# Three feed-forward blocks on the unnormed input instead of two, and the token mixer's loads and masks issued ahead of its layer norm

## The chip, the cores and the metric

The kernel is one program on one core of a Trainium2 chip. The metric is the time of one execution in microseconds (us). Weights come from HBM through the DMA queues while the core computes; TensorE (PE in the profile) does the matrix products, VectorE (DVE), ScalarE (ACT) and GpSimd (POOL) the elementwise work, SyncE (SP) issues most of the DMAs.

## The reference

One inference step of a decoder trunk with two layers, on 512 prompt positions and 8 x 4 sample positions, 544 columns in all, all in fp32. Cut to what matters here:

```
h = rmsnorm(x, norm1_g);  proj = h @ w_in            # 1024 -> 12 projections
A: gated delta rule     B: short gated convolution
C: out_c = window_attn_banded(cq, ck, cv, sinks)      # window 128, softmax with sinks
D: du  = gelu(d_u);  dvn = layernorm(gelu(d_v), d_ln_g, d_ln_b)
   wm  = where(tril, d_ws, 0)
   out_d = du * (einsum('gts,bcsgd->bctgd', wm, dvn) + d_bias)
x = x + concat(out_a, out_b, out_c, out_d) @ w_out
h2 = rmsnorm(x, norm2_g)
gate = causal_dwconv(h2 @ ffn_w_gate)                 # width 3, D_FF = 2816
x = x + (silu(gate) * (h2 @ ffn_w_up)) @ ffn_w_down
```

The states of the convolutions, the delta rule and the window caches are outputs too.

## The kernel before

**Numbers.** Activations lie with the channels on the 128 partitions and the 544 positions as columns. An fp32 product is made of three products of rounded parts: each operand is split into a high part (`xh`, `wh`) and a low part (`xl`, `wl`), and hi·hi, lo·hi and hi·lo are added in PSUM. A weight arrives as `wr`; ACT makes `wh` (L745), DVE makes `wl` (L747).

**Who sets the order.** PE's order is laid down when the program is built, by a planner (class `Order`). The main line yields after pieces of matrix products (`pj_*` are the projections); side generators yield a delay in microseconds, or an event that another one marks with a delay, and the planner, which adds up estimated PE time, takes whichever is due. The table `LAT` adds a delay to single steps of a generator. Side generators of layer l are `a` (delta rule), `c` (attention, `mix_c`), `d` (token mixing, `mix_d`), `e` (the sample positions' attention) and `n` (the layer norm of `dv`). The order of the other engines follows from a tile scheduler, so a step that moves on PE moves instructions on ACT and DVE as well.

**PSUM.** The pool `pss` has two buffers, which attention's scores (`psc`), its transposes (`ptr`), its products (`pov`), and token mixing's products (`pmx` for the prompt, `pmd` for the samples) take in turn. The pool `pmm` has two as well: projections, and in the feed-forward part `pgt` (gate) and `pup` (up) of one block after the other. A tile can be written again only when the last reader of the buffer's former content is done.

**Attention, one block of 128 queries.** PE writes the scores `psc`; DVE adds the mask (L1348), takes the maximum and its negative `nm` (L1254); ACT takes the exponentials (L1260) and, once the sum is inverted, scales (L1268); PE transposes into two tiles `ptr` (L441); ACT copies each to `pt` (L1363); PE multiplies with the values, `pov`.

**Token mixing (`mix_d`).** It waits for the event `dv{l}` (layer norm of `dv` done, `dvn` and `dvd` the results), loads the mixing weights `wmt`, masks them on POOL (L1379), loads and masks a small copy `wm4` (`wm`) for the samples (L1382), loads `dbias`, and then for each of two halves has PE multiply (`pmx`, `pmd`) and DVE add the bias and multiply with `du` (L1399).

**Feed-forward, 22 blocks of 128 channels per layer.** The first ones, `f < RAW`, use the input before the norm (`raw`): the products are made with the split `xs`, and the inverse norm `rstd` is multiplied in afterwards by DVE (L1713 and L1714 on the gate, L1716 before, and L1719 with the up product). Blocks up to 4 (`plain`) use the normed input in "forms": `fm.halves(kp)`, issued after block 0, makes the normed tiles `hn` (DVE, L578), and splits them into `f1h`, `f2h`, `f3h` (ACT, L586 and L515) and `f1l`, `f2l`, `f3l` (DVE, L587 and L516), for four values of kp; a plain block's gate goes from PSUM to SBUF by ACT (L1728, L1729), and its up product is multiplied in by DVE (L1734). Blocks from 5 on (`seven`) use seven products of half size where there would be eight, and for this need sums of the forms (`fm.sums()`: `fu`, `fv` on DVE, split into `f4`, `f5`), issued after block `RAW`.

Of the kernel before, what the change touches and what calls it, by code (L numbers as in the profile page):

```python
# [28 lines left out]
NK = DM // 128  # L29
EPS = 1e-6  # L30
FGROUPS = [(0, 5), (5, 11), (11, 17), (17, 22)]
RAW, PLAIN = 2, 5
P0 = 512 - HT


# [238 lines left out]
def _unhost(r):  # L274
# [8 lines left out]
    def conv(a, k, n):  # L283
# [19 lines left out]

LAT = {
    "a00": {
        3: 1.60, 13: 15.62, 14: 3.75, 15: 2.87, 16: 1.87, 17: 3.23, 18: 1.78, 19: 2.03, 34: 1.52,
    },
    "a01": {
        3: 3.96, 4: 1.12, 10: 2.64, 24: 0.84,
    },  # L310
    "a10": {
        3: 1.56, 13: 15.67, 14: 3.68, 15: 2.79, 16: 3.85, 17: 1.45, 25: 1.33, 36: 0.47, 42: 1.13,
    },
    "a11": {
        3: 3.59, 6: 3.32, 13: 1.06, 28: 0.70, 35: 0.30,
    },
    "c0": {
        1: 1.19, 2: 4.34, 5: 7.17, 6: 0.65, 7: 2.67, 8: 3.40,
    },
    "c1": {  # L320
        1: 0.81, 2: 4.06, 5: 7.68, 6: 0.61, 7: 15.38, 10: 1.48,
    },
    "d0": {
        4: 6.53,
# [90 lines left out]
def _body(ctx, tc, I, O, depth=DEPTH, dump=None):  # L415
# [7 lines left out]
    od = Order()  # L423

    def mm(out, lhsT, rhs, **kw):
        k, m, n = lhsT.shape[0], lhsT.free_size(), rhs.free_size()
        if lhsT.dtype == F32R:
            c = max(n, 256) / 2400.0 + 0.0025
        else:
            c = 4 * max(n, m) / 2400.0  # L430
            if k <= 32 and m <= 32:
                c *= 0.74
            elif k <= 64 and m <= 64:
                c *= 0.72
        od.spend(c, n * k / 128.0 * (1 if lhsT.dtype == F32R else 4))
        nc.tensor.matmul(out, lhsT, rhs, **kw)  # L436
# [9 lines left out]
    def bc(ap, axis, n):  # L446
        u = ap.unsqueeze(axis)
        shp = list(u.shape)
        shp[axis] = n
        return u.to_broadcast(shp)  # L450
# [16 lines left out]
    def n5(nm, w=571):  # L467
        return p5.tile([128, w], F32, tag="w5", name=nm)

    def nx(nm, shape, dt=F32):  # L470
        return slabs.tile(shape, dt, tag="s5", name=nm)

    def ncc(nm, shape):
        return pc.tile(shape, F32, tag="c2", name=nm)
# [4 lines left out]
    def ps(nm, shape):  # L479
        return pss.tile(shape, F32, tag="ps", name=nm)  # L480

    def psmm(nm):
        return pmm.tile([128, 1024], F32, tag="mm", name=nm)
# [16 lines left out]
    def C(nm, a=None, b=None):  # L500
        o, n = _COFF[nm]
        if a is None:
            return cst[:, o:o + n]
        return cst[:, o + a:o + b]
# [8 lines left out]
    def split(src, nm):  # L513
        hi, lo = nx(nm + "h", [128, T], F32R), nx(nm + "l", [128, T], F32R)
        act(hi, src, AF.Copy)  # L515
        tt(lo, src, hi.bitcast(F32), op=ALU.subtract)  # L516
        return hi, lo
# [232 lines left out]
    def wnext():  # L750
        while len(wready) < 3:
            n = len(wready)
            wprep()
            if len(wready) == n:
                break
        return wready.pop(0)
# [28 lines left out]
    def dmp(nm, ap):  # L785
        if dump is not None and nm in dump:
            nc.gpsimd.dma_start(dump[nm], ap)

    def bs(ap):
        return ap.rearrange("p (b t) -> p b t", b=DB)  # L790
# [582 lines left out]


    def mix_d(l, L):
        yield ("ev", f"dv{l}")
        wmt = nx("wmt", [128, 4, 128])
        nc.sync.dma_start(wmt, I["wmt"][l])
        pool.tensor_tensor(wmt, wmt, bc(C("tri"), 1, 4), op=ALU.mult)  # L1379
        wm4 = ncc("wm4", [32, 4, 32])  # L1380
        nc.sync.dma_start(wm4, I["wm4"][l])
        pool.tensor_tensor(wm4, wm4, bc(C("udc")[0:32], 1, 4), op=ALU.mult)  # L1382
        dbias = ncc("dbias", [128, 2, 128])
        nc.sync.dma_start(dbias, I["dbias"][l])
        for i in range(2):
            yield ("ev", f"u{l}{i}")
            pmx = ps("pmx", [128, 4, 128])
            for n in range(4):
                for a in range(2):
                    gr = 2 * i + a  # L1390
                    mm(pmx[hs[a], n], L.dvn[n // 2][:, n % 2, 64 * gr:64 * gr + 64], wmt[:, gr],
                       start=True, stop=True)
            pmd = ps("pmd", [128, ND])
            for a in range(2):
                gr = 2 * i + a
                mm(pmd[hs[a]], L.dvd[0:ND, 64 * gr:64 * gr + 64], wm4[:, gr], start=True, stop=True,
                   tile_position=(0, 64 * a))
            mx_ = n5("mx_", T)
            tt(mx_[:, 0:SEQ].rearrange("p (n t) -> p n t", n=4), pmx, bc(dbias[:, i], 1, 4), op=ALU.add)  # L1399
            tt(bs(mx_[:, SEQ:T]), bs(pmd), bc(dbias[:, i, 0:DS], 1, DB), op=ALU.add)  # L1400
            tt(mx_, mx_, L.du[i], op=ALU.mult)
            dmp(f"od{i}", mx_)
            L.cat[6 + i] = split(mx_, f"d{i}")
            yield 1.0
        od.mark(f"catD{l}", 3.5)


    def main():
# [7 lines left out]
        def xk(k):  # L1416
            return xr[k // 2][:, k % 2, :]
# [33 lines left out]
        for l in range(depth):  # L1451
# [53 lines left out]
            for c in range(5):  # L1505
# [5 lines left out]
                dv = dvn[c // 2][:, c % 2] if c < 4 else dvd[0:ND]  # L1511
# [15 lines left out]
            def normed_dv():  # L1527
                yield ("ev", f"nd{l}")
                with tc.issue_after(L.du_ins):
                    for c, (dv, r0) in enumerate(dvs):  # L1530
                        ts(dv, dv, mv[0:r0, c, 0:1], rs[0:r0, c:c + 1], op0=ALU.subtract, op1=ALU.mult)
                        pool.tensor_tensor(dv, dv, lnr[0:r0, 0], op=ALU.mult)
                        pool.tensor_tensor(dv, dv, lnr[0:r0, 1], op=ALU.add)
                nc.sync.dma_start(O["cvs"][l], dvd[0:ND])
                od.mark(f"dv{l}", 8.0)

            od.spawn(normed_dv(), f'n{l}')
            yield 0.0
# [165 lines left out]
            def raw(f, first):  # L1704
                p = psmm("pgt")
                yield from gemm(p, wnext(), xs)
                pu = psmm("pup")
                gu = gemm(pu, wnext(), xs)
                if first:
                    yield next(gu)  # L1710
                    nrm.finish()
                pb, dec = gate_in(f)
                tt(pb[:, 2:2 + SEQ], pflat(p, 0, SEQ), rstd[:, 0:SEQ], op=ALU.mult)  # L1713
                tt(dec[:, :, 2:6], bs(pflat(p, SEQ, T)), bs(rstd[:, SEQ:T]), op=ALU.mult)  # L1714
                sl = gate_out(f, pb, dec)
                tt(sl, sl, rstd, op=ALU.mult)  # L1716
                yield 0.0
                yield from gu
                tt(sl, sl, pflat(pu), op=ALU.mult)  # L1719
                hid[f] = split(sl, "hd")  # L1720
                yield 0.0

            def plain(f):

                p = psmm("pgt")
                yield from gemm_halves(p, wnext(), fm.whole())
                pb, dec = gate_in(f)
                act(pb[:, 2:2 + SEQ], pflat(p, 0, SEQ), AF.Copy)  # L1728
                act(dec[:, :, 2:6], bs(pflat(p, SEQ, T)), AF.Copy)  # L1729
                sl = gate_out(f, pb, dec)  # L1730
                yield 0.0
                pu = psmm("pup")
                yield from gemm_halves(pu, wnext(), fm.whole())
                tt(sl, sl, pflat(pu), op=ALU.mult)  # L1734
                hid[f] = split(sl, "hd")
                yield 0.0
# [37 lines left out]
            for kind, i, f0, f1 in FFN_ORDER:  # L1774
                if kind == "plain":
                    yield from raw(i, i == 0) if i < RAW else plain(i)
                    if i == 0:
                        for kp in range(NK // 2):
                            fm.halves(kp)
                    elif i == RAW:  # L1780
                        with tc.issue_after(fm.end.ins):
                            fm.sums()
                    continue
                if kind == "seven":
                    yield from seven(i)
                    continue
                m, last = i, f1 == NF
                hd = [hid[f] for f in range(f0, f1)]
                if last and l + 1 == depth and m >= NK - 2:
                    if m == NK - 2:  # L1790
                        yield from finale(xk, xr, nnrm, hd)
                    continue
                p = psmm("pdn")
                yield from gemm(p, wnext(), hd)
                tt(xk(m), xk(m), pflat(p), op=ALU.add)  # L1795
                if last:
                    if l + 1 < depth:
                        nx_xs.append(xsplit(xk(m), P(l + 1, "n1g", m, m + 1)))
                    nnrm.feed(m, xk(m))
                    if l + 1 == depth:  # L1800
                        act(xk(m), xk(m), AF.Copy, scale=fng[:, m:m + 1])
                yield 0.0
# [51 lines left out]
```

## Time and profile before

| | before |
|---|---|
| median of 3 runs | 1336.76 us (1336.02 to 1337.26) |
| profiled execution | 1336.89 us |
| its span in the trace | 1335.1 us |
| share of the span busy: PE, DVE, ACT, POOL | 97%, 72%, 48%, 30% |
| mean granted clock of PE | 0.99 of full speed |
| largest single wait of PE | 5.5 us, for `wmt` |

The profiled execution's time is 1.8 us longer than its span, and 0.13 us from the median. All rows below are of this execution. PE is busy nearly all of the span, so what can be gained without less arithmetic lies in the stretches in which PE waits, or in which it runs at a lower clock.

### The profile page before, as it was taken

The page shows a single profiled execution, that of the slowest core. Times are in us where ns is not written, and L with a number is a line of the kernel's source. Part 1 is how long each engine was busy: PE and PEld are TensorE (multiplying, and loading weights), DVE is VectorE, ACT ScalarE, POOL GpSimd, SP SyncE. Part 2 cuts the span into 40 slices and gives each one's busy share as a digit, 9 for nine tenths or more (in the row PEclk, how much of TensorE's full clock was granted, in tenths as well). Part 3 has the DMA queues.
Part 4 walks back from the last instruction along what each step waited for, and adds up shares of the span by engine and source line. Part 5 has one row for each costly group of instructions (what it writes and reads, how often), then busy time and mean ns, then how long its engine had stood idle before and what let it go on. Part 6 is the DMA issues. An engine that isn't in the chain of part 4 may idle for free.

```text
span 1335.1 us, 29979 instructions
## 1 busy us (share of the span) xinstructions
PE 1291.5 (97%) x12574; PEld 1240.5 (93%) x12574; DVE 958.9 (72%) x1565; ACT 647.2 (48%) x1142; POOL 401.9 (30%) x528
## 2 busy tenths in 40 slices
PE   8998999999999999999999989999999999999997
PEld 7987889999999999999999878889989999999997
DVE  6897943579777778876658867546796887687665
ACT  6645423455455444544545543335555454455444
POOL 2123320001655354452001142100034654643321
PEclk9998999998999999999999989999999999999999
DMA  7222241231233233233532221413312332232232
GB/s 279 99 69 65 80 133 42 89 101 58 70 101 101 84 100 102 84 95 88 162 124 101 66 75 60 124 46 98 99 52 87 92 111 86 97 99 88 89 91 73
DMA packets 48086, 125.60 MB, mean 94 GB/s; under 512 B 10144, under 2 KB 14432, under 8 KB 47824
## 3 DMA queue, kind: packets, MB, share of 16 engines
q1 hardware_dynamic: 47952, 123.70, 29.6%
q8 instruction: 98, 1.61, 0.5%
q14 instruction: 36, 0.29, 0.1%
HBM read 115.01 MB, written 8.67 MB: 93 GB/s over the span
## 4 chain that ended last, share of the span: by engine, by line
PE 81%; DVE 11%; ACT 3%; issue 2%; DMA 1%; POOL 0%; SPq 0%; DVEq 0%; ACTq 0%; POOLq 0%
PE pdn L436 17%; PE pA L436 11%; PE po L436 8%; PE pD L436 7%; PE pup L436 4%; PE pgt L436 4%; PE pB L436 4%; PE pC L436 3%; DVE wl L747 3%; PE ptm L436 2%; PE pj_b L436 2%; PE pj_z L436 2%; PE pj_c L436 2%; PE pj_h L436 2%; PE p L436 2%
## 5 line engine op out<-in xcount | busy, mean ns | idle before, releaser
L747 DVE TENSOR_TENSOR wl<-wr,wh 128x1024 fp32r<-128x1024 f32 (+4 forms) x218 | 257.6, 1182 | 91.0 <-ACT wh L745 89.7
L745 ACT ACTIVATE wh<-wr 128x1024 fp32r<-128x1024 f32 (+4 forms) x218 | 194.1, 890 | 197.6 <-PE pA L436 31.0
L436 PE MATMUL pdn<-hdh,wh 128*128 128x272 f32 x684 | 142.3, 289 | 8.3 <-DVE up L1769 3.7
L436 PE MATMUL pdn<-hdl,wh 128*128 128x272 f32 x684 | 141.7, 288 | 0.5 <-DVE hdl L516 0.5
L436 PE MATMUL pdn<-hdh,wl 128*128 128x272 f32 x684 | 141.2, 288 | 0.0
L745 ACT ACTIVATE wh<-s 128x1024 fp32r<-128x1024 f32 x68 | 72.0, 1058 | 99.9 <-PE pdn L436 90.1
L724 POOL TENSOR_TENSOR s<-wr 128x512 f32<-128x512 f32 x34 | 49.7, 1463 | 228.4 <-DMA wr<-w_u 122.7
L436 PEld LDWEIGHTS pdn<-hdh,wh 128*128 128x128 f32 x684 | 107.1, 188 | 10.2 <-issue 4.4
L436 PEld LDWEIGHTS pdn<-hdl,wh 128*128 128x128 f32 x684 | 107.3, 188 | 0.9 <-DVE hdl L516 0.9
L436 PEld LDWEIGHTS pdn<-hdh,wl 128*128 128x128 f32 x684 | 107.3, 188 | 0.0
L809 DVE SCALAR_TENSOR_TENSOR cacc<-pbf,prm,cacc 128x560 f32<-128x560 f32 x88 | 82.3, 936 | 34.0 <-ACT cacc L807 33.4
L747 DVE TENSOR_TENSOR wl<-s,wh 128x1024 fp32r<-128x1024 f32 x68 | 92.0, 1353 | 8.9 <-ACT wh L745 8.4
L1694 POOL COPY sfo<-pbf 128x2 f32<-128x2 f32 x44 | 27.9, 635 | 151.6 <-DVE pbf L1760 76.2
L1795 DVE TENSOR_TENSOR xr<-xr,pdn 128x544 f32<-128x544 f32 x62 | 44.4, 715 | 40.2 <-PE pdn L436 40.2
L725 POOL TENSOR_TENSOR s<-wr,s 128x512 f32<-128x512 f32 x34 | 62.2, 1831 | 0.9
L807 ACT ACTIVATE cacc<-pbf,prm 128x560 f32<-128x560 f32 x44 | 33.6, 765 | 50.4 <-DVE pbf L1761 45.9
L726 POOL TENSOR_TENSOR s<-wr,s 128x512 f32<-128x512 f32 x34 | 57.4, 1688 | 1.4
L727 POOL TENSOR_TENSOR s<-wr 128x512 f32<-128x512 f32 x34 | 56.7, 1668 | 0.0
L800 POOL MEMSET pbf<- 128x2 f32 x44 | 4.3, 97 | 158.6 <-DVE sq L536 153.6
L516 DVE TENSOR_TENSOR hdl<-sl,hdh 128x544 fp32r<-128x544 f32 x44 | 40.1, 911 | 5.2 <-ACT hdh L515 5.2
L1700 ACT ACTIVATE sl<-cacc 128x512 f32<-128x512 f32 x44 | 27.6, 628 | 32.7 <-DVE cacc L809 32.4
L436 PE MATMUL pA<-f5h,wh 128*128 128x272 f32 x136 | 39.3, 289 | 0.0
(636 smaller groups left out, 4180.4 us busy)
## 6 DMA issues: line engine op xcount, KB each, us to landing
wr<-w_g SPq DMA_DIRECT2D x44, 512.0 KB
wr<-w_u SPq DMA_DIRECT2D x44, 512.0 KB
wr<-w_ch SPq DMA_DIRECT2D x38, 512.0 KB
wr<-w_d SPq DMA_DIRECT2D x32, 384.0 KB
wr<-w_d SPq DMA_DIRECT2D x32, 320.0 KB
wr<-w_o SPq DMA_DIRECT2D x12, 384.0 KB
xr<-x_in SPq DMA_DIRECT2D x7, 544.0 KB
wr<-w_tm SPq DMA_DIRECT2D x8, 392.0 KB
```

Source lines behind the costliest of these rows:

```text
L436: nc.tensor.matmul(out, lhsT, rhs, **kw)
L516: tt(lo, src, hi.bitcast(F32), op=ALU.subtract)
L724: add(s12[:, lo_], u[:, lo_], u[:, hi_], op=ALU.add)
L725: add(s12[:, hi_], g[:, lo_], s12[:, lo_], op=ALU.add)
L726: add(s43[:, lo_], g[:, hi_], s12[:, hi_], op=ALU.add)
L727: add(s43[:, hi_], g[:, lo_], u[:, lo_], op=ALU.add)
L745: act(hi, r, AF.Copy)
L747: tt(lo, r, hi.bitcast(F32), op=ALU.subtract)
L807: act(acc[:, 0:out_n], pb[:, 0:out_n], AF.Copy, scale=wcol[:, 0:1])
L809: stt(acc[:, 0:out_n], pb[:, j:j + out_n], wcol[:, j:j + 1], acc[:, 0:out_n], op0=ALU.mult, op1=ALU.add)
L1694: pool.tensor_copy(sfo[:, f, 0:2], pb[:, SEQ:SEQ + 2])
L1795: tt(xk(m), xk(m), pflat(p), op=ALU.add)
```

## The change

`RAW` goes from 2 to 3: block 2 of each layer's feed-forward part works on the unnormed input, and blocks 3 and 4 stay plain. `fm.sums()` is still issued behind block 2. In `mix_d` the wait for `dv{l}` stands behind the three loads and the two masks, where it stood ahead of them; the event is marked with a delay of 11.0 where it was 8.0. Two steps of `LAT` get a larger delay (step 1 of `c0` and `c1`), and two get one that had none (step 12 of `a00` and `a10`).

```diff
-RAW, PLAIN = 2, 5
+RAW, PLAIN = 3, 5
...
 LAT = {
     "a00": {
-        3: 1.60, 13: 15.62, 14: 3.75, ...
+        3: 1.60, 12: 0.70, 13: 15.62, 14: 3.75, ...
     "a10": {
-        3: 1.56, 13: 15.67, 14: 3.68, ...
+        3: 1.56, 12: 0.70, 13: 15.67, 14: 3.68, ...
     "c0": {
-        1: 1.19, 2: 4.34, ...
+        1: 2.60, 2: 4.34, ...
     "c1": {
-        1: 0.81, 2: 4.06, ...
+        1: 2.30, 2: 4.06, ...
...
     def mix_d(l, L):
-        yield ("ev", f"dv{l}")
         wmt = nx("wmt", [128, 4, 128])
         nc.sync.dma_start(wmt, I["wmt"][l])
         pool.tensor_tensor(wmt, wmt, bc(C("tri"), 1, 4), op=ALU.mult)
...
         dbias = ncc("dbias", [128, 2, 128])
         nc.sync.dma_start(dbias, I["dbias"][l])
+        yield ("ev", f"dv{l}")
         for i in range(2):
...
-                od.mark(f"dv{l}", 8.0)
+                od.mark(f"dv{l}", 11.0)
...
-                    elif i == RAW:
+                    elif i == RAW - 1:
                         with tc.issue_after(fm.end.ins):
                             fm.sums()
```

The change moves instructions at three places that matter below. Inside `mix_d` the lines of the changed kernel are one lower (`wmt`'s load is L1377 there, its mask L1378); elsewhere they are the same.

**PE, layer 0, around the first `pmx`.** Before:

```order
L441 MATMUL ptr<-cst,sc 128x128 x8
L436 MATMUL pj_c_1561<-xh,wh 128x272 x2
L436 MATMUL pj_c_1561<-xl,wh 128x272 x2
L436 MATMUL pj_c_1561<-xh,wl 128x272 x2
L436 MATMUL pl_1574<-hvh,bonesr 128x512
L436 MATMUL pl_1574<-hvl,bonesr 128x512
L436 MATMUL pmx<-wmt,dvn_221 64x128 x4
L436 MATMUL pmx<-wmt,dvn_222 64x128 x4
L436 MATMUL pmd<-wm_1581,dvd 64x32 x2
L436 MATMUL pov<-pt,cv 64x256 x4
```

In the changed kernel (`pl` are sums over partitions for the norms of the delta rule's q and k; these tiles are in another pool):

```order
L436 MATMUL pj_c_1555<-xh,wh 128x272 x2
L436 MATMUL pj_c_1555<-xl,wh 128x272 x2
L436 MATMUL pj_c_1555<-xh,wl 128x272 x2
L436 MATMUL pl_1568<-hvh,bonesr 128x512
L436 MATMUL pl_1568<-hvl,bonesr 128x512
L441 MATMUL ptr<-cst,sc 128x128 x8
L436 MATMUL pj_c_1555<-xh,wh 128x272 x2
L436 MATMUL pj_c_1555<-xl,wh 128x272 x2
L436 MATMUL pj_c_1555<-xh,wl 128x272 x2
L436 MATMUL pmx<-wmt,dvn_221 64x128 x4
L436 MATMUL pmx<-wmt,dvn_222 64x128 x4
L436 MATMUL pmd<-wm_1343,dvd 64x32 x2
```

The transposes `ptr` stand later, behind `pl` and six products of `pj_c`, and another six of `pj_c` stand between them and `pmx`: twelve of `pj_c` instead of six are done ahead of `pmx`. Two `pl` and then `pov` follow `pmd`.

**ACT, the same place.** Before, from behind the exponentials:

```order
L1610 ACT_TABLE_LOAD
L1610 ACTIVATE du<-du 128x544
L1038 ACTIVATE Wc<-pW 128x256
ACT_TABLE_LOAD
L936 ACTIVATE sqd<-pl_1487,cst 128x32 x2
L943 ACTIVATE sqd<-sqd 128x64
L745 ACTIVATE wh<-wr 128x1024
L1363 ACTIVATE pt<-ptr 128x512
L1610 ACT_TABLE_LOAD
L1610 ACTIVATE du<-du 128x544
L1363 ACTIVATE pt<-ptr 128x512
ACT_TABLE_LOAD
```

In the changed kernel, from the second table load of this stretch on:

```order
ACT_TABLE_LOAD
L936 ACTIVATE sqd<-pl_1477,cst 128x32 x2
L943 ACTIVATE sqd<-sqd 128x64
L1268 ACTIVATE sc<-sc,es 128x256 x2
L745 ACTIVATE wh<-wr 128x1024
L1610 ACT_TABLE_LOAD
L1610 ACTIVATE du<-du 128x544
ACT_TABLE_LOAD
L942 ACTIVATE sql<-pl_1568,cst 128x512
L1363 ACTIVATE pt<-ptr 128x512
L945 ACTIVATE sql<-sql 128x512
L1363 ACTIVATE pt<-ptr 128x512
```

The scaling of the scores (L1268), which stood ahead of the first rows shown of before, stands behind `sqd`, and the first copy `pt` stands behind the second `du`, a further table load and L942, all of which followed it.

**DVE, feed-forward part, from block 1's L1716 on.** Before:

```order
L1716 TENSOR_TENSOR sl<-sl,rstd 128x544
L587 TENSOR_TENSOR f1l<-hn,f1h 128x272
L587 TENSOR_TENSOR f2l<-hn,f2h 128x272
L1719 TENSOR_TENSOR sl<-sl,pup 128x544
L516 TENSOR_TENSOR f3l<-hn,f3h 128x544
```

In the changed kernel:

```order
L1716 TENSOR_TENSOR sl<-sl,rstd 128x544
L587 TENSOR_TENSOR f1l<-hn,f1h 128x272
L587 TENSOR_TENSOR f2l<-hn,f2h 128x272
L1713 TENSOR_TENSOR pbf<-pgt,rstd 128x512
L1714 TENSOR_TENSOR pbf<-pgt,rstd 128x8x4
L1719 TENSOR_TENSOR sl<-sl,pup 128x544
L747 TENSOR_TENSOR wl<-wr,wh 128x1024
L516 TENSOR_TENSOR f3l<-hn,f3h 128x544
```

Block 2's L1713 and L1714 now stand between the forms and block 1's L1719, which is the last reader of block 1's `pup`.

## Rows read from the trace of the kernel before

**Rows 1.** The page: busy time by engine, granted clock in 40 slices.

```profile
PE 1291.5 (97%) x12574; PEld 1240.5 (93%) x12574; DVE 958.9 (72%) x1565; ACT 647.2 (48%) x1142; POOL 401.9 (30%) x528
...
PEclk9998999998999999999999989999999999999999
```

**Rows 2.** PE's waits: waiter and releaser: us in total, times, longest us.

```profile
PE pmx L436 <- POOL wmt L1379: 9.2, 2, 5.5
...
PE psc L436 <- DVE ck L1578: 2.7, 2, 1.4
```

**Rows 3.** Stretches of PE: window, us, busy (x), granted clock, DMA share, GB/s.

```profile
122.60:130.10 7.50, 7.06 (x99) 0.50 0.01 4
...
778.90:785.10 6.20, 5.24 (x82) 0.50 0.08 32
...
311.90:318.30 6.40, 6.10 (x25) 0.52 0.00 0
965.80:971.80 6.00, 4.61 (x28) 1.00 0.32 103
971.80:977.30 5.50, 4.32 (x23) 1.00 0.00 0
```

**Rows 4.** PE's timeline: the first `pmx` of each layer, idle and releaser in brackets.

```profile
122.60 1.98 PE L436 MATMUL pmx<-wmt,dvn 128*64 128x128 f32 x16 [5.54 <-POOL wmt L1379]
...
777.76 1.09 PE L436 MATMUL pmx<-wmt,dvn 128*64 128x128 f32 x16 [3.64 <-POOL wmt L1379]
```

**Rows 5.** Timeline of SP and POOL, layer 0: `wmt`'s load and mask, layer norm's end.

```profile
118.31 0.36 SPq L1378 DMA_DIRECT2D wmt<-wmt  x1
...
117.13 0.71 POOL L1533 TENSOR_TENSOR dvd<-dvd,lnr 32x256 f32<-32x256 f32 x1
121.28 1.26 POOL L1379 TENSOR_TENSOR wmt<-wmt,cst 128x512 f32<-128x512 f32 x1 [3.44 <-DMA wmt<-wmt]
```

**Rows 6.** ACT's timeline from the exponentials on, layer 0; last row, layer 1.

```profile
104.78 0.51 ACT L1260 ACTIVATE sc<-sc,nm 128x256 f32<-128x256 f32 x1 [1.31 <-DVE hvl L910]
...
107.92 1.28 ACT L1557 ACT_TABLE_LOAD   x1
109.22 0.63 ACT L1557 ACTIVATE vt<-cacc 128x512 f32<-128x512 f32 x1
...
115.94 0.58 ACT L1363 ACTIVATE pt<-ptr 128x512 f32<-128x512 f32 x1
...
118.00 0.66 ACT L1610 ACTIVATE du<-du 128x544 f32<-128x544 f32 x1 [0.18 <-DVE du L1607]
118.56 0.58 ACT L1363 ACTIVATE pt<-ptr 128x512 f32<-128x512 f32 x1
120.46 0.69 ACT L942 ACTIVATE sql<-pl,cst 128x512 f32<-128x512 f32 x1 [1.31 <-issue]
...
772.90 0.58 ACT L1363 ACTIVATE pt<-ptr 128x512 f32<-128x512 f32 x1
```

**Rows 7.** PE's timeline: first product of block 2's gate and up, layers 0 and 1.

```profile
305.87 0.29 PE L436 MATMUL pgt<-f1h,wh 128*128 128x272 f32 x1
...
318.10 0.29 PE L436 MATMUL pup<-f1h,wh 128*128 128x272 f32 x1
...
965.85 0.29 PE L436 MATMUL pgt<-f1h,wh 128*128 128x272 f32 x1
...
977.29 0.29 PE L436 MATMUL pup<-f1h,wh 128*128 128x272 f32 x1
```

**Rows 8.** The chain that ended last, in order of time: block 2's up.

```profile
318.26 6.01 PE pup L436 x48
```

**Rows 9.** DVE's timeline, layer 0: from block 1's L1719 to block 3's L1734.

```profile
312.43 0.71 DVE L1719 TENSOR_TENSOR sl<-sl,pup 128x544 f32<-128x544 f32 x1
313.06 0.71 DVE L516 TENSOR_TENSOR f3l<-hn,f3h 128x544 fp32r<-128x544 f32 x1
...
319.01 1.23 DVE L747 TENSOR_TENSOR wl<-wr,wh 128x1024 fp32r<-128x1024 f32 x1 [1.76 <-ACT wh L745]
...
338.82 0.71 DVE L1734 TENSOR_TENSOR sl<-sl,pup 128x544 f32<-128x544 f32 x1
```

**Rows 10.** DVE's groups, 299 to 340 us: busy us, mean ns of one, idle before.

```profile
L1716 DVE TENSOR_TENSOR sl<-sl,rstd 128x544 f32<-128x544 f32 x1 | 0.7, 709 | 0.0
...
L1713 DVE TENSOR_TENSOR pbf<-pgt,rstd 128x512 f32<-128x512 f32 x1 | 0.7, 684 | 0.0
```

More of the change, by code (lines that the diff above doesn't have):

```diff
@@ L305 @@
     "a00": {
-        3: 1.60, 13: 15.62, 14: 3.75, 15: 2.87, 16: 1.87, 17: 3.23, 18: 1.78, 19: 2.03, 34: 1.52,
+        3: 1.60, 12: 0.70, 13: 15.62, 14: 3.75, 15: 2.87, 16: 1.87, 17: 3.23, 18: 1.78, 19: 2.03, 34: 1.52,
     },
@@ L311 @@
     "a10": {
-        3: 1.56, 13: 15.67, 14: 3.68, 15: 2.79, 16: 3.85, 17: 1.45, 25: 1.33, 36: 0.47, 42: 1.13,
+        3: 1.56, 12: 0.70, 13: 15.67, 14: 3.68, 15: 2.79, 16: 3.85, 17: 1.45, 25: 1.33, 36: 0.47, 42: 1.13,
     },
@@ L317 @@
     "c0": {
-        1: 1.19, 2: 4.34, 5: 7.17, 6: 0.65, 7: 2.67, 8: 3.40,
+        1: 2.60, 2: 4.34, 5: 7.17, 6: 0.65, 7: 2.67, 8: 3.40,
     },
     "c1": {
-        1: 0.81, 2: 4.06, 5: 7.68, 6: 0.61, 7: 15.38, 10: 1.48,
+        1: 2.30, 2: 4.06, 5: 7.68, 6: 0.61, 7: 15.38, 10: 1.48,
     },
```

## The prediction

> **What bounds the kernel now.** The page comes first. PE is busy for 1291.5 of 1335.1 us [rows 1], so PE's order is the time, and a change that leaves PE's arithmetic alone can only gain what PE loses. Two kinds of loss are to be looked for: waits, and stretches at a lower clock, which the slices of the page's clock show as an 8 at three places [rows 1].
>
> The list of PE's waits comes next. Its largest entry is `pmx`, held back twice by POOL's mask on `wmt`, 9.2 us together [rows 2]. The timelines say where: 5.54 us ahead of 122.60 in layer 0, and 3.64 us ahead of 777.76 in layer 1 [rows 4]. In layer 0 the layer norm is done on POOL at 117.84, but `wmt` is only asked for at 118.31 on SP, and POOL masks it from 121.28 [rows 5]. The load is late because `mix_d` asks for it after the layer norm.
>
> Then the clock, in windows. Just after both waits the granted clock is 0.50, that is 1.2 GHz of 2.4, for 7.5 and 6.2 us [rows 3]. At half clock half of a stretch is lost, some 3.75 and 3.1 us. So the wait for `wmt` costs up to 5.54 + 3.64 + 6.85 = 16 us.
>
> The feed-forward part has the other loss. Block 2's gate, the first on the forms, starts at 305.87 and its up product at 318.10; in layer 1 at 965.85 and 977.29 [rows 7]. A chain of 48 such products takes 6.01 us undisturbed [rows 8]. So block 2's gate loses 12.23 - 6.01 = 6.2 us in layer 0 and 11.44 - 6.01 = 5.4 us in layer 1, since DVE makes the forms too slowly. In layer 0 part of it is a stretch at 0.52 [rows 3]; in layer 1, with much the same idle time (PE busy 4.61 of 6.0 and 4.32 of 5.5), the clock stayed at 1.00 [rows 3].
>
> **Feed-forward part.** A raw block 2 needs no forms for its gate, so the gate runs 305.87 to 311.9. Two waits follow, both read off DVE's order.
>
> Up of block 2 needs the buffer of block 1's up, which L1719 frees. Before, L1719 started at 312.43 [rows 9]; now L1713 (0.68 us [rows 10]) and a small L1714 stand ahead of it, some 0.7 us with their overlap. L1719 ends at 312.43 + 0.7 + 0.71 = 313.85, and PE waits 1.95 us.
>
> Up of block 4 needs the buffer of block 3's up, which L1734 frees. PE would want it four chains after 313.85, at 337.9. DVE went from the end of L1719 to the start of that L1734 in 338.82 - 313.06 = 25.76 us, 1.76 of it idle [rows 9]. Between these two places the changed order holds the same work and one L1716 more (0.71, about 0.64 with overlap [rows 10]). From 313.85 that gives an end of L1734 at 313.85 + 25.76 + 0.64 + 0.71 = 341.0 with all of the idle time, and at 339.2 with none. The wait is 3.1 or 1.3 us; I take 2.1, since DVE comes later to the place where it waited for ACT, and should wait less there.
>
> Up of block 3 wants its buffer at 325.9, and DVE's walk frees it at 325.7: no wait, with little to spare.
>
> Layer 0 gains 6.2 - 1.95 - 2.1 = 2.15 us, layer 1, where DVE's work is the same, 5.4 - 4.05 = 1.35. Sum **3.5 us**, between 1.5 and 5.1 by the two ends. ACT loses two small copies per layer, off the path.
>
> **Token mixing.** `wmt`, `wm4` and `dbias` are now asked for well ahead of the layer norm, behind an earlier slab of weights, and POOL masks them before it gets to the norm. POOL's 1.26 us for the mask come ahead of the norm, and if it waits for the load as it does now, another 3.44 us [rows 5]. The cover for this is the time between the norm's end, 117.84, and the 121.0 worked out below, 3.2 us; without it `pmx` would wait for the norm by up to 1.5 us. I take nothing, since the load is now asked for long before. On SP the three loads now go ahead of one output and one slab of weights; DMA is nearly idle behind the waits (shares of 0.01 and 0.08 [rows 3]), so the slab has room to come a little later, and I count it as nothing. So `wmt` is no longer late. What is late next?
>
> `pmx` and `pmd` take the buffers of the two `ptr` tiles, which ACT frees with its two `pt` copies. Before, the copies ended at 116.5 and 119.1 [rows 6], so that the first was hidden under the wait for `wmt`. In the changed order the first copy stands behind four more instructions: a table load (1.28), `du` (0.66), a table load (the 1.31 idle ahead of L942) and L942 (0.69) [rows 6], 3.94 us. The exponentials start with DVE's `nm`, ahead of which DVE's order puts three more instructions, but the scores lose their wait of 1.4 us [rows 2]; I let them start 0.4 us later. The copy then ends at 115.94 + 3.94 + 0.4 + 0.58 = 120.9. A second way to it: `du` waited for DVE's `du` until 118.00, and 118.00 + 0.66 + 1.31 + 0.69 + 0.58 = 121.2. I take 121.0. So `pmx` starts 1.6 us earlier than at 122.60, with six `pj_c` products (0.75 us at 6.01/48 each [rows 8]) more behind it: gain **2.35 us**.
>
> In layer 1 the same walk from 772.90 [rows 6] gives 772.90 + 3.94 + 0.4 + 0.58 = 777.8, by `du` about 778.3. `pmx` starts 0 to 0.5 us later than before, with six `pj_c` and two `pl` (1.35 us) more done: gain 0.9 to 1.35, and with the half-clock tail as uncertain as it is I take **0.9**. The ends of both together: 0, if the copies slip by another 1.6 us, and 9.2, all of the wait, if ACT's copies are in time.
>
> PE still idles some 3 to 4 us ahead of `pmx`. Idle times of 3.64 and 5.54 us were both followed by half clock [rows 3, 4], so I leave both half-clock stretches where they are.
>
> The waits for `psc` (2.7 us [rows 2]) go: the larger delays in the table put the scores behind six more products. But the time up to `pmx` is set by ACT, so this is only a longer wait there. Everything else that is reordered in the mixer is bounded by the waits that such places have now, 0 to 1.4 us each [rows 2]; I put one new wait of 1 us into each layer: **-2 us**.
>
> **The sum.** 3.5 + 2.35 + 0.9 - 2 = 4.75 us. From the profiled 1336.89 us, whose span has 1.8 us around it that stays, that gives 1332.1; this execution lies 0.1 above the median of the runs. Forecast **1332 us**. What a measurement of this kernel tells from no change is about 0.2%, 2.7 us.
>
> **A rule against the change.** ACT's table load at 107.92 takes 1.28 us, and the next instruction starts at 109.22, 0.02 us behind its end [rows 6]: a switch costs 1.3 us. If each cost about 1.4 us more, the two further switches ahead of `pt`, with the three there already, would put `pmx` some 7 us later than walked, in both layers, and the kernel would be at 1332 + 14 = 1346. The Trainium skill, "ScalarE: Activation LUTs", section "What ACT_TABLE_LOAD costs", gives a load of about 1283 ns and behind it a drain of about 1380 ns, 2.66 us for each switch. The trace agrees with the load and shows no drain. Chance 0.02.
>
> **Rivals.**
>
> *The copies are in time.* If ACT reaches `pt` before PE reaches `pmx`, the whole 9.2 us go, and with them both half-clock stretches (6.85): 3.5 + 16 - 2 = 17.5, time 1319. For it: the list of waits names `wmt` alone [rows 2]. Against it: the order of ACT, and `du`, which DVE gave out only at 118.00 [rows 6]. Chance 0.12.
>
> *No change.* Block 2's up waits 1.95 us in one piece. In layer 0 the clock fell in just this part of the program [rows 3]. If in both layers a fall of some 6 us follows that wait, it costs 2 x 3.1 = 6.2 us, and the sum is -1.5: 1338. With a fall in one layer it is +1.65: 1335.2. Against it: layer 1 idled 2.6 us of 11.5 at full clock [rows 3], in pieces. Chance 0.22, about 1336.5.
>
> *Slower.* Both feed-forward waits, in both layers, drop the clock: 4 x 3.1 = 12.4, sum -7.7, time 1344.5. It decides from the third fall on (sum -4.5, 1341.4). What speaks for it is only that waits of 3.64 us did so [rows 3, 4]; the 1.4 us of `psc` [rows 2] did not. Chance 0.10.
>
> **How the numbers follow.** My forecast, between 1328.5 and 1335.5 by the ends of its terms, has 0.54; the others 0.12, 0.22, 0.10 and 0.02. Faster by over 0.2% (below 1334.1): nine tenths of the forecast, the copies in time, and a little of no change, 0.63. Slower (above 1339.4): the last two and a little of no change, 0.14. The rest, 0.23, is the same. For 8 in 10 the range goes from 1321, which leaves most of the first rival out, to 1340.
>
> **What the profile of the changed kernel should show.** No wait of PE for `wmt`; in its place `pmx` waiting for ACT's `pt` by 3 to 4 us in layer 0, and the copy ending near 121. Half clock behind it. Block 2's gate in 6.0 us; block 2's up waiting about 2 us for DVE's L1719, block 4's up 1.3 to 3.1 us for L1734, at full clock. No `psc` wait for `ck`. The prediction is wrong if `pmx` doesn't wait, if the clock falls at the two feed-forward waits, or if a wait of over 2 us shows elsewhere in the mixer.

## The result

The changed kernel takes 1348.6 us (median of 4 runs, 1347.5 to 1353.0), the kernel before 1337.0. The ratio is 1.0092, with a 95% interval of 1.0071 to 1.0113: slower by 0.9%, where 1332 us, faster by 0.4%, was forecast. The profiled execution of the changed kernel is the slowest of its four, 1352.96 us, with a span of 1351.2. So in its trace there are 16 us to be found, of which the median has about 12.

### The profile page after: what moved, and what is told of

The parts are those of the page before. It is cut to its first block, busy times and chain, and to the rows that moved or that the text cites. A ratio compares the mean times of both kernels' runs of the same rounds, so it can differ in the third digit from the quotient of the medians.

```text
span 1351.2 us, 29998 instructions
## 1 busy us (share of the span) xinstructions
PE 1296.3 (96%) x12574; PEld 1247.5 (92%) x12574; DVE 970.2 (72%) x1571; ACT 646.7 (48%) x1138; POOL 398.0 (29%) x528
## 4 chain that ended last, share of the span: by engine, by line
PE 80%; DVE 11%; ACT 4%; issue 3%; DMA 1%; DVEq 0%; SPq 0%; ACTq 0%
PE pdn L436 17%; PE pA L436 10%; PE po L436 7%; PE pD L436 7%; PE pB L436 4%; PE pup L436 4%; DVE wl L747 3%; PE pC L436 3%; PE pgt L436 3%; PE pj_z L436 2%; PE pj_h L436 2%; PE ptm L436 2%; PE pj_u L436 2%; ACT wh L745 2%; PE p L436 2%
## 5 line engine op out<-in xcount | busy, mean ns | idle before, releaser
L1694 POOL COPY sfo<-pbf 128x2 f32<-128x2 f32 x44 | 25.0, 568 | 133.3 <-DVE pbf L1760 74.4
L802 POOL COPY pbf<-stf 128x16 f32<-128x16 f32 x44 | 33.8, 769 | 26.0 <-DMA stf<-stf 26.0
L1700 ACT ACTIVATE sl<-cacc 128x512 f32<-128x512 f32 x44 | 27.6, 627 | 28.5 <-DVE cacc L809 28.0
```

The lines of the kernel that those rows point to most:

```text
L802: pool.tensor_copy(dec[:, :, 0:e], st)
```

## The profile after

The page of the changed kernel: engines, and the granted clock in 40 slices.

```profile
PE 1296.3 (96%) x12574; PEld 1247.5 (92%) x12574; DVE 970.2 (72%) x1571; ACT 646.7 (48%) x1138; POOL 398.0 (29%) x528
...
PEclk9999899999999999999999988999999999999999
```

PE runs the same 12574 products as in [rows 1], and is busy 4.8 us longer, for half clock. The other 11.3 of the 16 us are idle time of PE (54.9 us, 43.6 before). The list of PE's waits:

```profile
PE pup L436 <- ACT pbf L1729: 6.6, 2, 3.3
...
PE pR L436 <- ACT Wc L1054: 4.6, 1, 4.6
PE pl L436 <- ACT sql L942: 4.4, 1, 4.4
PE pmx L436 <- ACT pt L1363: 4.2, 1, 4.2
PE py L436 <- DVE Y L1170: 3.9, 1, 3.9
PE pvt L436 <- DVE vnd L1225: 2.5, 1, 2.5
PE pup L436 <- DVE pbf L1714: 2.5, 2, 1.3
```

The 9.2 us for `wmt` and the 2.7 us for `ck` of [rows 2] are gone. In their place stand waits of 1.3 to 4.6 us each, and all but those of `pup` are in the mixer. Where they lie in time says PE's timeline (idle time and its releaser in brackets):

```profile
120.50 0.87 PE L436 MATMUL pmx<-wmt,dvn 128*64 128x128 f32 x6 [4.23 <-ACT pt L1363]
...
141.96 0.33 PE L436 MATMUL py<-Y,Nd 32*32 32x32 f32 x8 [3.93 <-DVE Y L1170]
...
174.56 0.65 PE L436 MATMUL pvt<-cst,vt 64*64 64x64 f32 x15 [2.52 <-DVE vnd L1225]
...
349.60 0.60 PE L436 MATMUL pup<-f1h,wh 128*128 128x272 f32 x1 [3.32 <-ACT pbf L1729]
...
786.97 0.80 PE L436 MATMUL pl<-hvh,bonesr 128*128 128x512 f32 x1 [4.40 <-ACT sql L942]
...
834.48 0.76 PE L436 MATMUL pR<-Wc,Tm 32*32 32x32 f32 x40 [4.56 <-ACT Wc L1054]
...
1016.35 0.39 PE L436 MATMUL pup<-f1h,wh 128*128 128x272 f32 x1 [3.33 <-ACT pbf L1729]
```

`pmx` in layer 0 does start earlier than in [rows 4], at 120.50 for 122.60. The loss comes behind it. In windows behind these waits (us, PE's busy time, granted clock, DMA) the clock shows what most of them cost once more:

```profile
120.50:125.00 4.50, 4.50 (x36) 0.62 0.16 64
142.00:148.00 6.00, 6.00 (x47) 0.51 0.01 3
158.00:162.00 4.00, 4.00 (x21) 0.57 0.00 0
174.60:178.00 3.40, 3.40 (x66) 0.59 0.28 51
350.00:353.00 3.00, 3.00 (x16) 0.55 0.57 146
788.00:797.00 9.00, 8.56 (x107) 0.53 0.03 11
834.50:841.00 6.50, 6.50 (x90) 0.52 0.04 12
...
1016.35:1020.00 3.65, 3.65 (x29) 1.00 0.44 141
```

Before, there were two such stretches in the mixers and one in the feed-forward part [rows 3]. Now a stretch near 1.2 GHz follows each wait of 2.5 us or more but one: behind block 4's up in layer 1, at 1016.35, the clock stayed at 1.00, though the same wait in layer 0 was followed by 0.55. And one stretch, from 158 us on, follows no wait: PE had been busy without a gap since 141.96.

The first product of certain tiles on PE in the traces, and by how much they come later (+) or earlier than in the kernel before, show where the time goes (us; the labels are those of the runs below):

```
               layer 0: pmx     po    pgt     pA   layer 1: pmx     po    pgt     pA
before               122.6  226.6  281.3  348.2          777.8  886.1  941.3 1007.3
changed kernel        -2.1   +8.9   +8.2   +8.9          +11.7  +16.1  +15.0  +15.2
mix_alone             -5.4   -7.0   -7.0   -7.3          -12.5  -14.7  -14.7  -12.0
order_alone           +1.1  +12.6  +12.0  +13.9          +20.2  +23.7  +22.6  +22.7
raw_alone             +1.0   +1.3   +1.3   +2.1           +1.9   +1.5   +1.6   +3.1
```

`po` is the first product behind the mixer, `pgt` the first of the feed-forward part, `pA` the first of block 5. In the changed kernel the mixer of layer 0 loses 11 us between `pmx` and `po`; the two feed-forward openings, `pgt` to `pA`, change by +0.7 and +0.2. The time is lost in the mixers: 8.9 us by `po` of layer 0, and 16.1 by `po` of layer 1.

## The experiments

Theory 1: the early loads are good, and the new order that the delays lay down on PE is what costs. Rivals: the third raw block costs; the early loads themselves cost; or whatever is won at `pmx` is given back behind it, since ACT and DVE pace the delta rule in any order.

**raw_alone**: only the third raw block.

```diff
-RAW, PLAIN = 2, 5
+RAW, PLAIN = 3, 5
...
-                    elif i == RAW:
+                    elif i == RAW - 1:
```

> The third raw block alone (RAW = 3, sums behind block 2), the mixer as before: PE's order in the mixer is that of the kernel before. The table of PE's progress of the changed kernel says that its feed-forward part gains some 4.5 us per layer by block 3 and loses them again, and a little more, at block 4's up product. Theory 1 (the loss of the changed kernel lies in the mixer, and the feed-forward part gives back what it gains): 1336 to 1338.5 us. Rival (the feed-forward part is faster by the predicted 3.5 us, and what is lost there is a consequence of the mixer): 1333 to 1334. Rival (the third raw block is the loss): above 1340.

Measured: 1337.8 us, ratio 1.0006 (0.9994 to 1.0017). No change that can be measured: the third raw block is not the loss, and not a gain either.

**mix_alone**: only the wait for `dv{l}` moved behind the loads and masks.

```diff
     def mix_d(l, L):
-        yield ("ev", f"dv{l}")
         wmt = nx("wmt", [128, 4, 128])
...
         nc.sync.dma_start(dbias, I["dbias"][l])
+        yield ("ev", f"dv{l}")
```

> Only the wait for the layer norm's event moved behind the loads and masks in the token mixing, delay 8.0 and the table as before, RAW = 2: PE's order is that of the kernel before, wmt is early. Theory 1 (early loads are good, the new order is what costs): pmx starts when the first pt copy is done, near 116.5 us in layer 0 and 773.5 in layer 1, some 5 and 3 us earlier than before, and at least a part of the half clock behind it goes: 1324 to 1331 us. Rival 2 (the loads on SP and the masks on POOL cost where they now stand, by delaying weights and the layer norm): 1337 or more. Rival 3 (every gain at pmx is given back within the delta rule, which ACT and DVE pace, whatever the order): 1335 to 1338.

Measured: 1323.8 us, ratio 0.990 (0.9886 to 0.9914), 12.9 us faster, just past the fast end of theory 1's range. Its PE timeline, layer 0:

```profile
117.17 1.09 PE L436 MATMUL pmx<-wmt,dvn 128*64 128x128 f32 x16
119.49 0.30 PE L436 MATMUL pmd<-wm,dvd 32*64 32x32 f32 x4 [1.23 <-ACT pt L1363]
```

`pmx` follows the products ahead of it without a wait, 5.4 us earlier than in [rows 4]. Behind it `pmd` waits 1.23 us for the second `pt`. The clock over the next 10 us, by window:

```profile
120.00:130.00 10.00, 9.37 (x186) 1.00 0.19 57
```

The half clock that stood here before is gone. The gain stays: -5.4 at `pmx`, -7.0 at `po` (table above). The rivals that the early loads cost, and that all of the gain is given back, fall.

**order_alone**: only the delays, with the loads late.

```diff
     "a00": {
+        12: 0.70,     (a10 too)
     "c0": {
-        1: 1.19,
+        1: 2.60,      (c1: 0.81 to 2.30)
...
-                od.mark(f"dv{l}", 8.0)
+                od.mark(f"dv{l}", 11.0)
```

> Only the delays: 11.0 instead of 8.0 for the layer norm's event, and the four entries of the table; loads and masks late as before, RAW = 2. PE's order in the mixer is that of the changed kernel. Theory 1: the waits behind pmx that the changed kernel shows (for Y, vnd, Wc, sql) are there again, and wmt may be late as well: 1347 to 1353 us. Rival 2: about 1337, since the loads stand as before. Rival 3: 1337 to 1340.

Measured: 1356.8 us, ratio 1.015 (1.0137 to 1.0163), 4 us slower than the range of theory 1, and far from both rivals. Its list of waits holds four of the changed kernel's in the mixer, and `wmt` besides:

```profile
PE pmx L436 <- POOL wmt L1379: 9.0, 2, 7.2
...
PE pl L436 <- ACT sql L942: 4.3, 1, 4.3
PE pR L436 <- ACT Wc L1054: 4.0, 1, 4.0
PE py L436 <- DVE Y L1170: 3.9, 1, 3.9
...
PE pvt L436 <- DVE vnd L1225: 2.5, 1, 2.5
```

These four waits belong to the order, and to nothing else in the change.

**mixer_part**: the changed kernel with `RAW` back at 2.

```diff
-RAW, PLAIN = 3, 5
+RAW, PLAIN = 2, 5
...
-                    elif i == RAW - 1:
+                    elif i == RAW:
```

> The changed kernel with RAW back at 2: moved wait, 11.0 and the table. Theory 1: all of the loss is here, 1346.5 to 1349.5 us, some 1 us less than the changed kernel. Rival (the third raw block is the loss): 1337 to 1340.

Measured: 1346.7 us, ratio 1.0077 (1.0065 to 1.0089). Against mix_alone the delays cost 1346.7 - 1323.8 = 22.9 us.

**early_mark11, early_table_c, early_table_a**: mix_alone with one of the three delays each (table entries abridged).

```diff
-                od.mark(f"dv{l}", 8.0)
+                od.mark(f"dv{l}", 11.0)                       (early_mark11)
...
-        1: 1.19 (c0), 1: 0.81 (c1)
+        1: 2.60 (c0), 1: 2.30 (c1)                            (early_table_c)
...
+        12: 0.70 (a00, a10)                                   (early_table_a)
```

> The early loads and masks with the event's delay 11.0 instead of 8.0, table as before. Two theories of what in the new order costs. Theory A: the later delay moves pmx, and all that stands behind it on PE, behind twelve more products of pj_c, but the steps between keep their distances: 1324 to 1330 us. Theory B: the two pmx, which take the two buffers that attention and the delta rule take in turn, now stand next to psc, ptr and pk, and hold these up: 1333 to 1345.

> The early loads and masks, delay 8.0, and of the table only step 1 of c0 and c1. Theory A (the later scores are what brings attention's steps onto the delta rule's): 1334 to 1345 us, half or more of the loss. Theory B (the loss is in the event's delay): 1321 to 1328, since the wait of psc for ck, 2.7 us in two, goes.

> The early loads and masks, delay 8.0, and of the table only step 12 of a00 and a10. Theory A: a delay of 0.7 us at one step moves later steps of the delta rule by little: 1322 to 1328 us. If the loss is in the delta rule's own order: 1333 to 1345.

Measured: 1329.6, 1330.2 and 1334.8 us (ratios 0.9936, 0.9940 and 0.9978, each within 0.0025). Against mix_alone's 1323.8 that is +5.8, +6.4 and +11.0, together 23.2, beside the 22.9 us of the three at once. For early_mark11 the figure lies in theory A's range, near its upper end. For early_table_c it lies between the two ranges, so that neither theory holds. For early_table_a the "small" theory is wrong: the smallest delay, 0.7 us at one step of the delta rule, costs most.

That the three add up so closely is no proof that the costs are independent. The kernel before ran 1 us slower beside these three than beside mix_alone; by the ratios the parts are some 4.8, 5.3 and 10.4, together some 20.5, for 23.7 of the three at once. And the waits are not the same ones. None of the four waits above appears at 1.2 us or more with one delay alone; early_table_a, for one, has these at the head of its list:

```profile
PE ptr L441 <- DVE sc L1270: 5.5, 2, 3.3
PE pmd L436 <- ACT oc L1371: 3.5, 2, 2.4
```

So the four waits belong to the delays together, not to one of them.

**early_table_c_less** and **early_mark9_5**: the c delays shortened to 0.40 and 0.10, and the event's delay at 9.5, both on mix_alone.

```diff
-        1: 1.19 (c0), 1: 0.81 (c1)
+        1: 0.40 (c0), 1: 0.10 (c1)                            (early_table_c_less)
...
-                od.mark(f"dv{l}", 8.0)
+                od.mark(f"dv{l}", 9.5)                        (early_mark9_5)
```

> The early loads and masks with the delays of step 1 of c0 and c1 made shorter (0.40 and 0.10) instead of longer, all else as before. Early loads alone: 1323.8 us; with the longer delays of the changed kernel 1330.2. Theory A (the order before is a tuned one, and a shift either way lays steps of attention and delta rule onto each other): 1327 to 1335 us. Theory B (the longer delay is wrong as such, shorter is better or the same): 1319 to 1325.

> The early loads and masks with the event's delay at 9.5, between 8.0 (1323.8 us) and 11.0 (1329.6). Theory A (each order has its own accidents): anywhere from 1323 to 1335, not bound to lie between. Theory B (later is worse in proportion): 1326 to 1328.

Measured: 1334.3 us (ratio 0.9982, 0.9968 to 0.9996) and 1327.3 us (0.9927, 0.9901 to 0.9952). Shorter costs 10.5 us where longer cost 6.4, as theory A has it: for step 1 of `c0` and `c1` the order before is better than one on either side of it. The 9.5 lies between 8.0 and 11.0, as "later is worse in proportion" has it too; with runs from 1324.6 to 1329.7 this one doesn't tell the theories apart, and its loss against mix_alone is not clear of the noise.

**early_raw3** and **early_raw3_sums_later**: mix_alone with the third raw block, and the sums behind block 2 or behind block 3. The second one's whole difference to the kernel before is below; the first has also `elif i == RAW - 1`, as the changed kernel does.

```diff
-RAW, PLAIN = 2, 5
+RAW, PLAIN = 3, 5
...
     def mix_d(l, L):
-        yield ("ev", f"dv{l}")
...
         nc.sync.dma_start(dbias, I["dbias"][l])
+        yield ("ev", f"dv{l}")
```

> The early loads and masks with the order as before, three raw blocks, but the sums of the forms issued behind block 3 instead of block 2. In the run with the third raw block alone, PE had gained 5.2 us in layer 0 when block 2's gate was done, and lost it again at block 4's up product (3.3 us) and in the half clock behind it, because DVE made the sums ahead of the conv that ACT's copy of the gate waits behind. Theory 1 (it is the place of the sums): that wait goes, 1315 to 1320 us. Rival (DVE's work up to block 5 is too much wherever it stands): the wait moves to block 5's products on the sums, 1322 to 1326.

> The changed kernel without its delays: early loads and masks, three raw blocks, sums behind block 2, the event's delay 8.0 and the table as before. If the parts add up (early loads -12.9 us, third raw block +1.2): 1325 us, 1323.5 to 1327. Beside the run with the sums behind block 3 (1317.6) it says what the place of the sums is worth.

Measured: early_raw3 1324.8 us (0.9915, 0.9889 to 0.9941), as the parts add up; early_raw3_sums_later **1317.6 us** (0.9845, 0.9829 to 0.9861), the fastest of all, 19 to 20 us below the kernel before. Block 4's up no longer waits there. The first entries of its waits:

```profile
PE pdn L436 <- DVE up L1769: 3.5, 4, 1.1
PE psc L436 <- DVE ck L1578: 2.7, 2, 1.4
PE pup L436 <- DVE pbf L1714: 2.5, 2, 1.3
```

No wait is over 1.4 us, and PE's busy time is 11.4 us less than in [rows 1] for the same products:

```profile
PE 1280.1 (97%) x12574; PEld 1234.1 (94%) x12574; DVE 964.8 (73%) x1571; ACT 644.8 (49%) x1138; POOL 411.6 (31%) x528
```

In every stretch of 5 us in which PE worked the granted clock was 1.00. So of the 20.2 us by which its span is shorter than before, 11.4 are half clock that is gone, and 8.8 idle time.

**changed_sums_later**: the changed kernel with the sums behind block 3.

```diff
-                    elif i == RAW - 1:
+                    elif i == RAW:
```

> The changed kernel with one edit: the sums of the forms issued behind block 3 instead of block 2. The same edit, with the third raw block, took 6.2 us off the kernel with early loads. If feed-forward part and mixer are independent, the changed kernel loses its wait of 3.3 us at block 4's up in both layers, and the half clock behind it: 1340 to 1343 us. If not: 1346 to 1350.

Measured: 1340.7 us, ratio 1.0026 (1.0014 to 1.0039), 7.9 us less than the changed kernel. On the kernel with early loads the same edit took 7.2 us: as far as these two pairs show, the place of the sums is worth about the same with either mixer.

## Why the prediction was wrong

**The step that failed** is the last one of the token mixing: "Everything else that is reordered in the mixer is bounded by the waits that such places have now ... I put one new wait of 1 us into each layer: -2 us." In the changed kernel three such places (`py`, `pvt`, `pR`) wait 2.5 to 4.6 us, 11.0 us together, and half clock follows each. The mixer as a whole was forecast 2.35 + 0.9 - 2 = 1.25 us faster, and mixer_part measures it 10.1 us slower (1346.7 for 1336.7): if the other two terms are left as they stand, the -2 should have been about -13. (The 22.9 us of the delays against mix_alone are more, since they hold as well what the late copies cost at `pmx`, which the prediction had counted.) So of the 16.6 us by which the forecast missed, 11.3 are the mixer's and 4.7 the feed-forward part's (below). Waits of an order that was adapted to these latencies do not bound those of another order.

`py` in layer 0 shows how. It needs `Y`, which DVE makes from `pkd`. PE's order from one to the other, in the kernel before and so in mix_alone (counts are the program's; the traces have two records for each of the small products, such as `py`):

```
pkd x12
L436 MATMUL pj_h_1865<-xh,wh 128x272 x2      (6 products of pj_h in 3 rows; then 6 more)
L436 MATMUL pk<-kq_424 64x128 x8
L436 MATMUL pR<-Wc,Tm 32x32 x32
                                             (6 of pj_h)
L441 MATMUL ptr<-cst,sc 128x128 x8
                                             (6 of pj_h)
L436 MATMUL py<-Y,Nd 32x32 x4
```

and in the changed kernel:

```
pkd x12
L436 MATMUL pW<-R,N 32x32 x32
                                             (6 of pj_h)
L436 MATMUL py<-Y,Nd 32x32 x4
```

In mix_alone `pkd` starts at 132.81 on PE, and `Y` is ready at 139.03 + 0.18 on DVE, 6.4 us later; `py` starts at 139.67 without a wait (PE and DVE, timelines):

```profile
132.81 0.24 PE L436 MATMUL pkd<-kq 64*32 64x64 f32 x1
...
139.67 0.26 PE L436 MATMUL py<-Y,Nd 32*32 32x32 f32 x8
...
139.03 0.18 DVE L1170 TENSOR_TENSOR Y<-Y,cst 128x32 f32<-128x32 f32 x1
```

In the changed kernel:

```profile
135.45 0.30 PE L436 MATMUL pkd<-kq 64*32 64x64 f32 x2 [1.37 <-DVE mx__1796 L1399]
...
140.57 1.25 DVE L1170 TENSOR_TENSOR Y<-Y,cst 128x32 f32<-128x32 f32 x1
...
140.03 1.73 POOL L971 TENSOR_TENSOR qk<-qk,cst 128x512 f32<-128x512 f32 x1
```

From `pkd` at 135.45 to `Y` at 140.57 + 1.25 it is again 6.4 us. The way through DVE has the same length, in part by chance: DVE's order between the two differs as well, and the last step, L1170, took 1.25 us beside POOL's L971 where it took 0.18 in mix_alone. What changed is that PE has only 2.6 us of work between the two (135.45 to 138.03, where its idle time begins) instead of 6.9. It waits the other 3.9 us, and then runs 6 us at 0.51. That the other waits of the list arise in the same way is argued from the fact that order_alone has them too; it was not measured for each. Which steps of the three delays set each of them off together stays open.

**Right in mechanism.** `wmt` is no longer late, and `pmx` in layer 0 waits for ACT's first `pt`, whose end was forecast for 120.9 to 121.2. It ended at 119.77 + 0.59 = 120.36:

```profile
119.19 0.69 ACT L942 ACTIVATE sql<-pl,cst 128x512 f32<-128x512 f32 x1 [1.31 <-issue]
119.77 0.59 ACT L1363 ACTIVATE pt<-ptr 128x512 f32<-128x512 f32 x1
```

So the wait, 4.23 us, is a little over the forecast 3 to 4, and half clock does follow. In layer 1 the wait moved one step up, to `pl`, for the L942 that stands ahead of `pt` (4.40 us), with 9 us at 0.53 behind it. The rival "the copies are in time" came true for the order of the kernel before, where the copies stand earlier: mix_alone gained 12.9 of the 16 us that the prediction put on the wait for `wmt`. So the early loads by themselves are worth four times the 3.25 us that the prediction gave to both `pmx`; in the changed order the late copies take most of that away.

**The feed-forward part** was forecast at -3.5 us and measured at +1.2 (raw_alone), no change clear of noise. This term failed too. Block 2's gate no longer waits, as forecast. But the walk took the wrong PSUM buffer, twice. Block 2's up waits for L1714, so it takes the buffer of its own block's gate, and waits 1.3 us, not the 1.95 for L1719. Block 4's up waits for ACT's copy of its own gate, L1729, for 3.3 us, not the 2.1 for L1734, with half clock behind it in layer 0 (0.55 for 3 us above) and none in layer 1. So the clock fell behind one of these four waits (two up products, two layers), where the forecast had none and the rival *Slower* all four. L1719 and L1734 can't be the releasers: they ended behind the starts of the two up products (322.10 for 321.62, 352.13 for 349.60). The timelines of raw_alone show why that copy is late; ACT first:

```profile
340.32 0.63 ACT L1700 ACTIVATE sl<-cacc 128x512 f32<-128x512 f32 x1
...
341.93 0.57 ACT L1728 ACTIVATE pbf<-pgt 128x512 f32<-128x512 f32 x1
```

L1728 stands behind L1700, which waits for a conv (`cacc`) that ends on DVE at 339.44 + 0.79. DVE and POOL ahead of it:

```profile
329.95 1.53 DVE L607 TENSOR_TENSOR fv<-hn 128x272 f32<-128x272 f32 x1
331.41 1.82 DVE L516 TENSOR_TENSOR f4l<-fu,f4h 128x544 fp32r<-128x544 f32 x1
...
337.74 0.43 DVE L607 TENSOR_TENSOR fv<-hn 128x272 f32<-128x272 f32 x1
338.10 0.71 DVE L516 TENSOR_TENSOR f4l<-fu,f4h 128x544 fp32r<-128x544 f32 x1
339.44 0.79 DVE L809 SCALAR_TENSOR_TENSOR cacc<-pbf,prm,cacc 128x560 f32<-128x560 f32 x1
...
329.70 1.49 POOL L724 TENSOR_TENSOR s<-wr 128x512 f32<-128x512 f32 x1
331.14 1.50 POOL L727 TENSOR_TENSOR s<-wr 128x512 f32<-128x512 f32 x1
```

Two things come together: the conv stands behind the sums (`fu`, `fv`, `f4`) in DVE's order, and four DVE instructions among those take 1.5 to 1.8 us instead of 0.43 and 0.71 while POOL runs, 4.4 us more in all. With the sums one block later the conv comes first, and the wait is gone; this the runs show. POOL's disturbance alone does not make the wait. In early_raw3_sums_later it hits DVE just as hard, at the conv and the first sums:

```profile
320.78 3.56 DVE L809 SCALAR_TENSOR_TENSOR cacc<-pbf,prm,cacc 128x560 f32<-128x560 f32 x2 [0.20 <-ACT cacc L807]
324.26 3.68 DVE L599 TENSOR_TENSOR fu<-hn 128x272 f32<-128x272 f32 x4
```

In the kernel before the same two rows take 1.64 and 1.49 us. DVE loses 4.1 us here, and block 4's up does not wait. Whether the wait would be there without POOL was not measured.

The `psc` wait is gone, as forecast; that this is no gain was not measured by itself. The parts as measured, each by itself: early loads -12.9 us (mix_alone), delays +22.9 on top of these (mixer_part), third raw block +1.2 (raw_alone, not clear of noise), together +11.2 us; the changed kernel has +11.6.

Of the prediction's own signs of being wrong two came: waits of over 2 us elsewhere in the mixer, and a fall of the clock behind a feed-forward wait. The rival *Slower*, with 1344.5 us, comes near the measured time by chance: of its four falls of the clock in the feed-forward part one came, and the loss lies in the mixer, where it had none.

## What to carry to other kernels

Where an order is written from a table of delays, each delay stands for a latency on other engines, and the work between a step and the step that needs its result is the cover for it. Before a shift, walk the distance between each producer and consumer that it moves, not only the one place that it is meant for. Changes in one diff are to be run one by one; here the moved wait alone was worth -12.9 us and lay hidden under +22.9. And a tile's PSUM buffer is whichever its pool gives out: read from the waits of the built order which reader frees it, before its wait is priced.

## What the hardware showed

DVE's adds and subtracts of two SBUF operands took up to 3.6 times as long while POOL did the same kind of work: `fv` 1.53 us for 0.43, `f4l` 1.82 for 0.71, each about as long as one POOL instruction (1.49 to 1.50) beside it. The Trainium skill, "SBUF — State Buffer", section "Who interferes with whom", says that a DVE instruction with two SBUF inputs contends with a GpSimd instruction that reads SBUF, and that the shared port pair is an exclusive lock. The trace agrees. The prediction took DVE's time from the kernel before, where the sums ran undisturbed (`fv` 0.43 us each).

Whether the clock falls behind a wait can't be read from the length of the wait in these runs. In the changed kernel it stayed at 1.00 behind 3.33 us (layer 1) and fell behind 3.32 us for the same instruction (layer 0). In mix_alone it stayed at 1.00 behind the 1.23 us of `pmd`. In early_raw3, at the same place, `pmd` waited 1.03 us, and soon after PE ran at 0.50:

```profile
118.84 0.30 PE L436 MATMUL pmd<-wm,dvd 32*64 32x32 f32 x4 [1.03 <-ACT pt L1363]
...
121.00:124.00 3.00, 3.00 (x73) 0.50 0.36 141
```

What a fall costs can be read: a window's length, times what its clock lacks of 1.00. The stretches of the changed kernel shown above cost 1.4 to 4.2 us each. That is why early_raw3_sums_later, in which the clock stayed up throughout, gains more than the idle time that it removes.
